# Two attention blocks in one kernel: scores of even and odd heads issued in turn into two PSUM banks, and one PSUM pool of eight banks

## The chip, the cores and the metric

The kernel runs on one core of a Trainium2 chip. Times are device microseconds of one launch; the time of a kernel is the median of its runs. The engines are TensorE (PE in the profile, with its weight loads as PEld), VectorE (DVE), ScalarE (ACT), GpSimd (POOL) and SyncE (SP), which here issues the loads. PSUM, into which PE writes its products, has eight banks of 128 x 512 float32.

## The reference

The input x has 256 tokens of width 1024. Two residual networks run one after the other, each with two layers; all of it is float32.

```python
def first_block(x, ...):
    for l in range(2):
        x = x + 0.5 * swiglu(rms_norm(x, norm_ffn1[l]), ...)
        x = x + hybrid_mixer(rms_norm(x, norm_mix[l]), ...)   # 12 dilated softmax heads, 4 stick-breaking heads
        x = x + 0.5 * swiglu(rms_norm(x, norm_ffn2[l]), ...)
    return rms_norm(x, norm_final)

def second_block(x, ...):
    for l in range(2):
        proj = rms_norm_2(x, norm_mix_pre[l]) @ w_in[l]
        # o_a: attention over compressed, selected and windowed keys (8 heads)
        # o_b: conformer, 31 taps, layer norm; o_c: pooling; o_d: sliding-window attention with sinks (8 heads)
        up = einsum("bsnc,ncd->bsnd", stack([o_a, o_b, o_c, o_d]), w_branch[l])
        mix = einsum("bsnd,bsnd->bsd", sigmoid(h @ w_gate[l]), up) @ w_o[l]
        x = x + rms_norm_2(mix, norm_mix_post[l])
        x = x + rms_norm_2(gated_conv_ffn(rms_norm_2(x, norm_ffn_pre[l])), norm_ffn_post[l])
    return x
```

A head has 64 features. Per 128 queries a softmax head needs the scores q k^T (with a mask), their maximum, the exponential, and the product with v.

## The kernel before

The tokens are two tiles of 128 (t = 0, 1). Every weight is loaded as float32 in chunks of 128 x 1024 (`chunk`), which ACT rounds to `wh` (L110) and DVE completes by `wl` (L111); a product with a weight is three matmuls into a tile called `lin`: L184 to L186 (`mm3`, 128 x 512) or L203 to L205 (`lin_T`, 128 x 256). `kouter` runs the products with the down and output weights, half of the columns after the other; behind each half stands the residual or the norm, and `head` makes `xg`, x times the gain of the next norm (L1026), which `transposed` turns by four matmuls with the identity (L155).

Everything else that PE does goes into tiles called `aux`: transposes, scores, products with v, statistics. An attention (`attend1` in the first block, `attn` in the second, where `AHEAD` lets the scores run two groups ahead of the outputs) works by heads: the mask by a bf16 matmul (L415, L458, L519 to L523), the score products (L421, L464, L527; for the compressed keys L810), DVE's maximum (L423, L530), ACT's exponential (L432, L539), transposes of `e` (L155), a copy to SBUF (L436, L547), the products with v (L449, L553). A head's 64 features of q and k lie on partitions 0 to 63 if the head is even and 64 to 127 if it is odd; a score product so uses 64 rows of PE's array (64*128 in the rows below) where all others use 128.

The program is written in one sequence, layer by layer. A scheduler of the tile framework decides the order on each engine: it starts an instruction when what it needs is there, and it gives a tile a buffer of its tag in the order in which the program asks for it. PSUM has two tags, four banks each:

```python
psum = ctx.enter_context(tc.tile_pool(name="psum", bufs=4, space=bass.MemoryType.PSUM))
psum.tile([P, 512], F32, tag="lin", name=nm("lin"))
psum.tile([P, 512], F32, tag="aux", name=nm("aux"))
```

So `lin` tiles that stand later in the program can be filled while `aux` tiles of an attention wait for DVE or ACT. The functions that the change touches, with what calls them:

Of the kernel before, what the change touches and what calls it, by code (L numbers as in the profile page):

```python
# [8 lines left out]
F32 = mybir.dt.float32  # L9
# [6 lines left out]
P = 128  # L16
# [9 lines left out]
def body(tc, ctx, I, C, out, upto=99):  # L26
# [9 lines left out]
    psum = ctx.enter_context(tc.tile_pool(name="psum", bufs=4, space=bass.MemoryType.PSUM))  # L36
# [14 lines left out]
    def lin_ps():  # L51
        return psum.tile([P, 512], F32, tag="lin", name=nm("lin"))

    def aux_ps():
        return psum.tile([P, 512], F32, tag="aux", name=nm("aux"))
# [47 lines left out]
    # ---- weights: float32 as loaded, split into two float32r parts that add up to it  # L103
# [63 lines left out]
    def split_T(tag, srcs, scale=None):  # L167
        """[128 tokens, 512] blocks -> XT of their transposes (one or two blocks)."""
# [25 lines left out]
    def lin_T(xts, ws, blks, ps=None, ks=range(8)):  # L194
        """Transposed products: [128 columns of the weights, all tokens] blocks, two to a PSUM bank."""
# [12 lines left out]
    def row_scale(xts):  # L208
        """The tokens' 1/rms along the free axis, on every partition."""
# [71 lines left out]
    class Halves:  # L281
        """XT of both token tiles, split half by half as the blocks come."""
# [9 lines left out]
    # ---- block 1  # L292
    def ffn1(xts, tail, wg, wu, wd):
        hts = [XT(), XT()]
        rb = None
        for nb in range(6):
# [9 lines left out]
            else:  # L306
                # the first half of the features first: the other half's norm may still be under way
# [71 lines left out]
    def attend1(qkn, vs):  # L379
        QT = [None, None]  # L380
        oTs = []
        for t in range(2):
# [26 lines left out]
            for j in range(4):  # L409
                groups = [[0, 1, 2]] if t == 0 else [[0, 1], [2]]  # L410
                ps_l, mx, sm = [], stat(4), stat(4)
                for gi, gs in enumerate(groups):
                    n = len(gs) * nk * P
                    ps = aux_ps()[:, :n]
                    nc.tensor.matmul(ps, identb, dilm[t][:, gs[0]:gs[-1] + 1, :].rearrange("p g k -> p (g k)"),  # L415
                                     start=True, stop=False)
                    for gg in gs:
                        h = gg * 4 + j
                        for kt in range(nk):
                            c0 = ((gg - gs[0]) * nk + kt) * P  # L420
                            nc.tensor.matmul(ps[:, c0:c0 + P], qk(h, False, t), qk(h, True, kt), start=False,  # L421
                                             stop=(gg == gs[-1] and kt == nk - 1))
                    V.tensor_reduce(mx[:, gi:gi + 1], ps, op=OP.max, axis=AX.X)  # L423
                    ps_l.append(ps)
# [26 lines left out]
            # stick-breaking heads, keys on partitions: log w = z - sum over j >= s of softplus(z_j)  # L451
# [3 lines left out]
            for par in range(2):  # L455
                o = par * 64
                z = aux_ps()[:, :n]
                nc.tensor.matmul(z[:, n - 256:], identb, sbm[:, None, :].to_broadcast([P, 2, P]), start=True, stop=False)  # L458
                for kt in range(nk):
                    for jj in range(2):  # L460
# [3 lines left out]
                        nc.tensor.matmul(z[:, c0:c0 + P], k_, q_, start=False, stop=(kt == nk - 1 and jj == 1))  # L464
                S.activation(es[par], z, AF.Abs)
                zs.append(z)
# [39 lines left out]
    def attn(t, qT, kTf, vf, window, sink=None):  # L506
        """softmax attention of 8 heads over the keys up to the query; returns the unnormalised output and the sums."""
# [4 lines left out]
        def scores(h0):  # L512
            par = h0 % 2
            hs = list(range(h0, h0 + 2 * per, 2))
            n = per * nk * P
            ps = aux_ps()[:, :n]
            pv = ps.rearrange("p (h k) -> p h k", h=per)
            if t == 0:
                nc.tensor.matmul(pv, identb, swm[:, None, P:].to_broadcast([P, per, P]), start=True, stop=False)  # L519
            elif window:  # L520
                nc.tensor.matmul(pv, identb, swm[:, None, :].to_broadcast([P, per, 2 * P]), start=True, stop=False)
            else:
                nc.tensor.matmul(pv[:, :, P:], identb, swm[:, None, P:].to_broadcast([P, per, P]), start=True, stop=False)  # L523
            for i, h in enumerate(hs):
                q_ = qT[par * 64:par * 64 + 64, (h // 2) * P:(h // 2 + 1) * P]
                for kt in range(nk):
                    nc.tensor.matmul(pv[:, i, kt * P:(kt + 1) * P], q_, kTf(kt, h), start=False,  # L527
                                     stop=(i == per - 1 and kt == nk - 1))
            sl = slice(h0, h0 + 2 * per - 1, 2)
            V.tensor_reduce(mx[:, sl], pv, op=OP.max, axis=AX.X)  # L530
            if sink is None:
                V.tensor_scalar(ng[:, sl], mx[:, sl], -0.125, None, op0=OP.mult)  # L532
            else:
                V.scalar_tensor_tensor(mx[:, sl], mx[:, sl], 0.125, sink[:, sl], op0=OP.mult, op1=OP.max)
                V.tensor_scalar(ng[:, sl], mx[:, sl], -1.0, None, op0=OP.mult)
            e = unit("e")[:, :n]
            ev = e.rearrange("p (h k) -> p h k", h=per)
            for i, h in enumerate(hs):
                S.activation(ev[:, i], pv[:, i], AF.Exp, bias=ng[:, h:h + 1], scale=0.125, accum_out=dn[:, h:h + 1])  # L539
            return h0, e  # L540
# [14 lines left out]
        # the scores run one group ahead of the outputs  # L555
        ahead = []
        po = None
        for par in range(2):
            for h0 in range(par, 8, 2 * per):
                ahead.append(scores(h0))  # L560
                if po is None:
                    po = aux_ps()
                if len(ahead) > AHEAD:
                    output(*ahead.pop(0))
# [15 lines left out]
    def mixer2(xts, tail, l):  # L580
# [8 lines left out]
        # pooling branch  # L589
# [45 lines left out]
        # token blocks for the compressed keys and values  # L635
# [22 lines left out]
        # conformer branch: gated input, transposed, 31 taps  # L658
# [15 lines left out]
        # compressed keys and values  # L674
# [35 lines left out]
        # projections of the attention branches  # L710
# [17 lines left out]
        # compressed keys (transposed) and values (block diagonal over the heads)  # L728
# [23 lines left out]
        # rotated keys, on both halves of the partitions  # L752
# [29 lines left out]
        # sliding window with sinks  # L782
# [13 lines left out]
        # native sparse attention: compressed, selected and window parts  # L796
        oA = []
        for t in range(2):
# [8 lines left out]
            for par in range(2):  # L807
                ps = aux_ps()[:, :64].rearrange("p (i n) -> p i n", i=4)
                for i in range(4):
                    nc.tensor.matmul(ps[:, i], qu[par * 64:par * 64 + 64, i * P:(i + 1) * P],  # L810
                                     kcT[par * 64:par * 64 + 64, (i // 2) * 16:(i // 2) * 16 + 16],
                                     start=i == 0, stop=i == 3)
                V.tensor_tensor(sc[:, par], ps, cmpm[t][:, None, 0:16].to_broadcast([P, 4, 16]), op=OP.add)
# [27 lines left out]
        def conformer():  # L841
            # convolution along the tokens (channels on partitions)
# [7 lines left out]
            # layer norm over the channels and silu of the conformer branch  # L850
# [27 lines left out]
        # gated sum of the branches  # L878
# [37 lines left out]
    def ffn2(xts, tail, l):  # L916
# [6 lines left out]
        for nb in range(6):  # L923
# [9 lines left out]
            for which in range(2):  # L933
# [8 lines left out]
                for t in range(0 if nb else 2):  # L942
                    # by token tiles, so that the second one's norm may still be under way
# [31 lines left out]
    # ---- the chain of sublayers: each ends, per token tile, with the norm that opens the next one  # L975
# [113 lines left out]
def layouts(inputs):  # L1089
    """Small per-channel parameters laid out with the channels on partitions."""  # L1090
# [44 lines left out]
```

## Time and profile before

| what | us |
|---|---|
| median of 3 runs (2186.62 to 2187.11) | 2186.66 |
| span of the profiled execution | 2183.6 |
| PE busy in it | 2154.8 |
| DVE busy | 1498.1 |
| ACT busy | 1111.1 |
| POOL busy | 37.2 |

The profiled execution is told by its span, from the first instruction to the end; the timed runs lie 3.1 us above it, in what stands around the span. A float32 matmul of 128 columns appears as two instructions in the trace (two passes), so counts of score products and of transposes are twice those of the code.

### The profile page before, as it was taken

The numbers are of one execution on the slowest core, as the hardware profiler recorded it, in microseconds if no ns is written. First come the engines' busy times: TensorE is split into PE (matmuls) and PEld (weight loads), VectorE is DVE, ScalarE is ACT, GpSimd is POOL, SyncE is SP. The second block draws the span as 40 slices with busy tenths as digits, with TensorE's granted clock in tenths as the row PEclk, the third lists the DMA queues.
The fourth block names the chain that finished last, engine by engine and source line by source line (L and its number), as shares of the span: only waits on it lengthen the run. The fifth ranks groups of instructions, "written<-read, shape, count | busy, mean of one in ns | idle before, by whom it ended". The sixth has DMA issues, their size and how long they took to land.

```text
span 2183.6 us, 33552 instructions
## 1 busy us (share of the span) xinstructions
PE 2154.8 (99%) x13232; PEld 1900.9 (87%) x13232; DVE 1498.1 (69%) x2219; ACT 1111.1 (51%) x1590; POOL 37.2 (2%) x55
## 2 busy tenths in 40 slices
PE   7999999999999999999999999999999999999998
PEld 7998888999899888889987888888987888888997
DVE  5665456665566555476657997668976898577983
ACT  4444545444444455544445654447655554446662
POOL 0000000000000000000000000000000000000000
PEclk9999999999999999999999999999999999999999
DMA  8656534665665654366566642456666743355653
GB/s 258 184 186 181 193 115 127 185 190 184 194 183 174 198 186 146 94 195 182 172 199 188 213 132 86 134 176 207 182 192 198 210 139 118 110 183 173 185 176 124
DMA packets 210126, 374.02 MB, mean 171 GB/s; under 512 B 15024, under 2 KB 42032, under 8 KB 209968
## 3 DMA queue, kind: packets, MB, share of 16 engines
q1 hardware_dynamic: 209392, 371.48, 55.3%
q8 instruction: 104, 1.70, 0.3%
q0 software_dynamic: 576, 0.39, 0.1%
q14 instruction: 54, 0.44, 0.1%
HBM read 371.17 MB, written 1.05 MB: 170 GB/s over the span
## 4 chain that ended last, share of the span: by engine, by line
PE 95%; DVE 3%; POOL 1%; issue 1%; ACT 1%; DMA 0%; SPq 0%; POOLq 0%; DVEq 0%
PE lin L186 17%; PE lin L184 17%; PE lin L185 17%; PE lin L203 11%; PE lin L204 11%; PE lin L205 11%; PE aux L155 4%; PE aux L527 2%; PE aux L553 1%; PE aux L421 1%; DVE wl L111 1%; PE aux L449 1%; DVE xg L1026 0%; POOL st L255 0%; DMA x<-in_x_dram 0%
## 5 line engine op out<-in xcount | busy, mean ns | idle before, releaser
L111 DVE TENSOR_TENSOR wl<-raw,wh 128x1024 fp32r<-128x1024 f32 (+1 forms) x688 | 834.9, 1217 | 467.6 <-ACT wh L110 459.0
L110 ACT ACTIVATE wh<-raw 128x1024 fp32r<-128x1024 f32 (+1 forms) x688 | 723.5, 1055 | 672.8 <-PE lin L186 325.0
L203 PE MATMUL lin<-hi,wh 128*128 128x256 f32 x1984 | 563.0, 284 | 0.0
L204 PE MATMUL lin<-lo,wh 128*128 128x256 f32 x1984 | 562.6, 284 | 0.0
L205 PE MATMUL lin<-hi,wl 128*128 128x256 f32 x1984 | 562.2, 283 | 0.0
L186 PE MATMUL lin<-wh,lo 128*128 128x512 f32 (+2 forms) x1376 | 536.1, 390 | 1.5 <-DVE rs L1037 0.9
L184 PE MATMUL lin<-wh,hi 128*128 128x512 f32 (+2 forms) x1376 | 536.7, 391 | 0.0
L185 PE MATMUL lin<-wl,hi 128*128 128x512 f32 (+2 forms) x1376 | 534.6, 389 | 1.5 <-DVE wl L111 1.5
L204 PEld LDWEIGHTS lin<-lo,wh 128*128 128x128 f32 x1984 | 381.8, 192 | 0.2
L203 PEld LDWEIGHTS lin<-hi,wh 128*128 128x128 f32 x1984 | 381.8, 192 | 0.2
L205 PEld LDWEIGHTS lin<-hi,wl 128*128 128x128 f32 x1984 | 381.6, 192 | 0.0
L186 PEld LDWEIGHTS lin<-wh,lo 128*128 128x128 f32 x1376 | 258.6, 188 | 54.1 <-DVE lo L147 2.6
L185 PEld LDWEIGHTS lin<-wl,hi 128*128 128x128 f32 x1376 | 258.7, 188 | 51.3 <-DVE wl L111 1.9
L184 PEld LDWEIGHTS lin<-wh,hi 128*128 128x128 f32 x1376 | 258.6, 188 | 50.7 <-ACT wh L110 0.4
L847 DVE SCALAR_TENSOR_TENSOR cy<-cT,pm,cy 128x251 f32<-128x251 f32 (+17 forms) x240 | 101.4, 463 | 0.2
L959 DVE SCALAR_TENSOR_TENSOR fy<-fu,fc,fy 128x255 f32<-128x255 f32 (+1 forms) x176 | 72.0, 477 | 0.2
L186 PE MATMUL lin<-wh,fl 128*128 128x512 f32 x176 | 68.6, 390 | 0.0
L184 PE MATMUL lin<-wh,fh 128*128 128x512 f32 x176 | 68.5, 389 | 0.0
L185 PE MATMUL lin<-wl,fh 128*128 128x512 f32 x176 | 68.5, 389 | 0.0
L539 ACT ACTIVATE e<-aux,st 128x128 f32<-128x128 f32 (+1 forms) x96 | 39.0, 422 | 42.3 <-DVE st L532 30.0
L255 POOL TENSOR_TENSOR st<-st,half 128x1 f32<-128x1 f32 x28 | 27.4, 979 | 1674.8 <-DVE st L254 1673.5
L957 ACT ACTIVATE fy<-fu,fc 128x256 f32<-128x256 f32 x88 | 45.7, 589 | 0.6 <-DVE fu L941 0.6
(303 smaller groups left out, 1956.9 us busy)
## 6 DMA issues: line engine op xcount, KB each, us to landing
raw<-in_ffn_w_up_dram SPq DMA_DIRECT2D x160, 512.0 KB, 4.1
raw<-in_ffn_w_down_dram SPq DMA_DIRECT2D x132, 512.0 KB, 4.3
raw<-in_w_in_dram SPq DMA_DIRECT2D x132, 512.0 KB, 4.0
raw<-in_ffn_w_gate_dram SPq DMA_DIRECT2D x80, 512.0 KB, 4.3
raw<-in_w_gate_dram SPq DMA_DIRECT2D x64, 512.0 KB, 3.9
raw<-in_w_branch_dram SPq DMA_DIRECT2D x32, 512.0 KB, 4.6
raw<-in_ffn_w_up_dram SPq DMA_DIRECT2D x32, 256.0 KB, 3.3
raw<-in_w_out_dram SPq DMA_DIRECT2D x16, 512.0 KB, 4.2
```

The source lines that it names most:

```text
L110: S.activation(wh, raw, AF.Copy)
L111: V.tensor_sub(wl, raw, wh.bitcast(F32))
L155: nc.tensor.transpose(p[:, i * P:(i + 1) * P], s, ident)
L184: nc.tensor.matmul(ps, xt.h[k], w[0], start=start, stop=False)
L185: nc.tensor.matmul(ps, xt.h[k], w[1], start=False, stop=False)
L186: nc.tensor.matmul(ps, xt.l[k], w[0], start=False, stop=stop)
L203: nc.tensor.matmul(o, wh, xh, start=k == 0 and i % 2 == 0, stop=False)
L204: nc.tensor.matmul(o, wh, xl, start=False, stop=False)
L205: nc.tensor.matmul(o, wl, xh, start=False, stop=k == 7 and i % 2 == 1)
L847: V.scalar_tensor_tensor(y4[:, c, sh:], c4[:, c, :T - sh], cw[:, j * 4 + c:j * 4 + c + 1], y4[:, c, sh:], op0=OP.mult, op1=OP.add)
L957: S.activation(y4[:, c], u4[:, c], AF.Identity, scale=fc[:, f0 + 2:f0 + 3], bias=fc[:, f0 + 3:f0 + 4])
L959: V.scalar_tensor_tensor(y4[:, c, sh:], u4[:, c, :T - sh], fc[:, f0 + 2 - sh:f0 + 3 - sh], y4[:, c, sh:], op0=OP.mult, op1=OP.add)
```

## The change

The two tags become one with eight buffers. In all attentions the score products of two groups of heads, an even and an odd one, are issued in turn, each group into a bank of its own; before, a group was finished before the next was begun. In the first block a pair of heads (j = 0, 1 and j = 2, 3) has both its scores made first, and then goes through exponential, transposes, copy and output one after the other. The number of products is the same.

```diff
-    psum = ctx.enter_context(tc.tile_pool(name="psum", bufs=4, space=bass.MemoryType.PSUM))
+    psum = ctx.enter_context(tc.tile_pool(name="psum", bufs=8, space=bass.MemoryType.PSUM))
     def lin_ps():
-        return psum.tile([P, 512], F32, tag="lin", name=nm("lin"))
+        return psum.tile([P, 512], F32, tag="ps", name=nm("lin"))
     def aux_ps():
-        return psum.tile([P, 512], F32, tag="aux", name=nm("aux"))
+        return psum.tile([P, 512], F32, tag="ps", name=nm("aux"))
...
+            def scores(js):
+                r = [([], stat(4), stat(4)) for _ in js]
                 for gi, gs in enumerate(groups):
                     n = len(gs) * nk * P
-                    ps = aux_ps()[:, :n]
-                    nc.tensor.matmul(ps, identb, dilm[t][:, gs[0]:gs[-1] + 1, :].rearrange("p g k -> p (g k)"),
-                                     start=True, stop=False)
+                    pss = [aux_ps()[:, :n] for _ in js]
+                    for ps in pss:
+                        nc.tensor.matmul(ps, identb, dilm[t][:, gs[0]:gs[-1] + 1, :].rearrange("p g k -> p (g k)"),
+                                         start=True, stop=False)
                     for gg in gs:
                         for kt in range(nk):
                             c0 = ((gg - gs[0]) * nk + kt) * P
+                            for ps, j in zip(pss, js):
+                                h = gg * 4 + j
+                                nc.tensor.matmul(ps[:, c0:c0 + P], qk(h, False, t), qk(h, True, kt), start=False,
+                                                 stop=(gg == gs[-1] and kt == nk - 1))
...
+            for js in ((0, 1), (2, 3)):
+                for j, r in zip(js, scores(js)):
+                    output(j, *r)
...
-            for i, h in enumerate(hs):
-                q_ = qT[par * 64:par * 64 + 64, (h // 2) * P:(h // 2 + 1) * P]
+            for i in range(per):
                 for kt in range(nk):
+                    for par, pv in enumerate(pvs):
+                        h = h0 + 2 * i + par
+                        q_ = qT[par * 64:par * 64 + 64, (h // 2) * P:(h // 2 + 1) * P]
+                        nc.tensor.matmul(pv[:, i, kt * P:(kt + 1) * P], q_, kTf(kt, h), start=False,
+                                         stop=(i == per - 1 and kt == nk - 1))
```

The stick-breaking heads and the compressed keys (L810 before) are changed in the same way. The order on PE, at the first head of the first layer's attention (query tile 0; lin_3029 is a tile of the gates' product, which stands behind the attention in the program). Before:

```order
L421 MATMUL aux_2624<-qt_2595 128x128 [waits Activation_49]
L421 MATMUL aux_2624<-qt_2596,qt_2595 128x128 [waits DVE_49]
L421 MATMUL aux_2624<-qt_2596,qt_2595 128x128
L186 MATMUL lin_3029<-wh_3007,lo_1845 128x512
L184 MATMUL lin_3029<-wh_3007,hi_1844 128x512
L185 MATMUL lin_3029<-wl_3008,hi_1844 128x512
L186 MATMUL lin_3029<-wh_3007,lo_1845 128x512
L184 MATMUL lin_3029<-wh_3013,hi_1844 128x512
L185 MATMUL lin_3029<-wl_3014,hi_1844 128x512
L186 MATMUL lin_3029<-wh_3013,lo_1845 128x512
L184 MATMUL lin_3029<-wh_3013,hi_1844 128x512
L155 MATMUL aux_2633<-ident,e_2631 128x128 [waits Activation_49]
```

The same place after the change (aux_2626 is head 0's bank, aux_2627 head 1's):

```order
L425 MATMUL aux_2626<-qt_2595 128x128 [waits DVE_49,Activation_49]
L425 MATMUL aux_2627<-qt_2595 128x128
L425 MATMUL aux_2626<-qt_2596,qt_2595 128x128 [waits DVE_49]
L425 MATMUL aux_2627<-qt_2596,qt_2595 128x128
L425 MATMUL aux_2626<-qt_2596,qt_2595 128x128
L425 MATMUL aux_2627<-qt_2596,qt_2595 128x128
L155 MATMUL aux_2641<-ident,e_2639 128x128 [waits Activation_49]
L155 MATMUL aux_2641<-ident,e_2639 128x128 x2
L457 MATMUL aux_2648<-v_2117,pt_2645 128x64 [waits DVE_49]
L457 MATMUL aux_2648<-v_2117,pt_2645 128x64 x2
L155 MATMUL aux_2656<-ident,e_2654 128x128 [waits Activation_49]
L155 MATMUL aux_2656<-ident,e_2654 128x128 x2
```

Between the scores and the transposes of `e` that need their exponential stood eight `lin` matmuls; now none stands there, nor between the transposes and the products with v. It is so in all four attentions: from the first transposes of q and k to the last of the output PE's order holds no `lin` matmul (186 matmuls of the code in a row in each layer of the first block, 294 in each of the second).

The order on PE behind the first half of the first sublayer's down product (the transposes of xg for the next sublayer; lin_1871 and lin_1872 are the second half of the columns). Before:

```order
L184 MATMUL lin_1872<-wh_1875,hi_438 128x512 [waits PE_49]
L185 MATMUL lin_1872<-wl_1876,hi_438 128x512
L155 MATMUL aux_1848<-ident,xg_1846 128x128 [waits DVE_49]
L155 MATMUL aux_1848<-ident,xg_1846 128x128 x3
L186 MATMUL lin_1872<-wh_1875,lo_439 128x512
L155 MATMUL aux_1861<-ident,xg_1859 128x128 [waits DVE_49]
```

After:

```order
L185 MATMUL lin_1641<-wl_1705,hi_1630 128x512
L186 MATMUL lin_1641<-wh_1704,lo_1631 128x512
L155 MATMUL aux_1848<-ident,xg_1846 128x128 [waits DVE_49,PE_49]
L155 MATMUL aux_1848<-ident,xg_1846 128x128 x3
L155 MATMUL aux_1861<-ident,xg_1859 128x128 [waits DVE_49,PE_49]
L155 MATMUL aux_1861<-ident,xg_1859 128x128 x3
L184 MATMUL lin_1871<-wh_1875,hi_438 128x512 [waits Activation_49]
```

The eight matmuls of the second half that stood ahead of the transposes now stand behind them, and the transposes follow the last matmul on whose product xg depends (lin_1641).

The order on PE at the layer norm of the conformer, second block, first layer (L860 and L867 before are L881 and L888 after). Before:

```order
L184 MATMUL lin_13305<-wh_13315,hl_12039 128x512
L860 MATMUL aux_13278<-avg,sq_13276 128x1 [waits PE_49,Activation_49]
L860 MATMUL aux_13278<-avg,sq_13276 128x1 x7
L185 MATMUL lin_13305<-wl_13316,hl_12039 128x512
L186 MATMUL lin_13305<-wh_13315,hl_12039 128x512
L867 MATMUL aux_13291<-ident,st_13289 128x128 [waits PE_49,Pool_49]
```

After:

```order
L186 MATMUL lin_13120<-wh_13090,lo_10950 128x512
L874 MATMUL aux_13270<-cy_11353,avg 128x256 x4
L881 MATMUL aux_13278<-avg,sq_13276 128x1 [waits Activation_49]
L881 MATMUL aux_13278<-avg,sq_13276 128x1 x7
L888 MATMUL aux_13291<-ident,st_13289 128x128 [waits Pool_49]
L888 MATMUL aux_13291<-ident,st_13289 128x128
L184 MATMUL lin_13305<-wh_13309,hl_12039 128x512
```

The three steps of the statistics follow each other directly; 16 `lin` matmuls stood between the first and the second, two between the second and the third.

## Rows read from the trace of the kernel before

**Rows 1.** The page: span, busy times, and TensorE's granted clock in 40 slices.

```profile
span 2183.6 us, 33552 instructions
...
PE 2154.8 (99%) x13232; PEld 1900.9 (87%) x13232; DVE 1498.1 (69%) x2219; ACT 1111.1 (51%) x1590; POOL 37.2 (2%) x55
...
PEclk9999999999999999999999999999999999999999
...
L255 POOL TENSOR_TENSOR st<-st,half 128x1 f32<-128x1 f32 x28 | 27.4, 979 | 1674.8 <-DVE st L254 1673.5
```

**Rows 2.** The waits of PE over the span: total us, times, longest us.

```profile
PE aux L155 <- DVE xg L1026: 15.0, 9, 7.6
PE aux L749 <- POOL hv L745: 2.3, 2, 1.4
```

**Rows 3.** Windows over one attention stretch of each block: busy us of every engine.

```profile
272.00:353.00 81.00, 81.00 (x467) 65.19 (x466) 41.51 (x86) 42.15 (x71) 0.00 (x0) 1.00 0.34 104
...
1257.00:1378.00 121.00, 120.91 (x729) 99.78 (x728) 99.02 (x218) 62.26 (x153) 0.00 (x0) 1.00 0.33 105
```

**Rows 4.** The same two windows, instructions on aux tiles alone: PE, PEld, DVE, ACT.

```profile
272.00:353.00 81.00, 43.09 (x295) 34.60 (x280) 19.81 (x39) 16.04 (x41) 1.00 0.34 104
...
1257.00:1378.00 121.00, 62.07 (x452) 50.48 (x434) 27.26 (x44) 30.81 (x114) 1.00 0.33 105
```

**Rows 5.** Timeline of one head of query tile 0: start, us, engine, line.

```profile
280.34 0.48 PE L421 MATMUL aux<-qt 64*128 64x128 f32 x2
280.66 0.61 PE L421 MATMUL aux<-qt,qt 64*128 64x128 f32 x4
...
281.31 0.56 DVE L423 TENSOR_REDUCE st<-aux 128x1 f32<-128x384 f32 x1 [0.74 <-PE aux L421]
...
282.15 0.58 ACT L432 ACTIVATE e<-aux,st 128x384 f32<-128x384 f32 x1 [4.28 <-DVE st L427]
...
282.94 0.49 PE L155 MATMUL aux<-ident,e 128*128 128x128 f32 x3
...
283.47 0.56 DVE L436 COPY pt<-aux 128x384 f32<-128x384 f32 x1 [0.45 <-PE aux L155]
...
284.20 0.78 PE L449 MATMUL aux<-v,pt 128*128 128x64 f32 x6
```

**Rows 6.** Groups by line and form, window 272 to 353 (first block's attention).

```profile
L436 DVE COPY pt<-aux 128x512 f32<-128x512 f32 x4 | 2.8, 692 | 4.4 <-PE aux L155 4.4
L423 DVE TENSOR_REDUCE st<-aux 128x1 f32<-128x512 f32 x4 | 2.7, 687 | 1.8 <-PE aux L421 1.8
...
L468 ACT ACT_TABLE_LOAD x2 | 2.6, 1283 | 0.0
L475 ACT ACT_TABLE_LOAD x2 | 2.6, 1283 | 0.0
...
L467 ACT ACTIVATE se<-se 128x1024 f32<-128x1024 f32 x1 | 1.1, 1059 | 0.0
```

**Rows 7.** Groups by line and form, window 1257 to 1378 (second block's attentions).

```profile
L527 PE MATMUL aux<-kT,qT 64*128 64x128 f32 x96 | 14.4, 287 | 0.0
...
L539 ACT ACTIVATE e<-aux,st 128x256 f32<-128x256 f32 x24 | 11.1, 470 | 15.3 <-DVE st L532 9.2 <-PE aux L155 3.5 <-DVE st L534 2.6
L539 ACT ACTIVATION_READ_ACCUMULATOR e<-aux,st 128x1 f32 x48 | 9.9, 206 | 0.0
...
L530 DVE TENSOR_REDUCE st<-aux 128x2 f32<-128x512 f32 x12 | 8.3, 689 | 4.4 <-PE aux L527 4.4
```

**Rows 8.** The chain that ended last, two of its pieces: start, us, what.

```profile
307.73 1.08 PE aux L421 x8
...
322.43 1.42 PE aux L449 x12
```

**Rows 9.** Windows around the conformer's statistics: busy us of PE, PEld, DVE, ACT, POOL, then the granted clock.

```profile
1393.00:1397.00 4.00, 3.54 (x26) 2.83 (x25) 0.85 (x2) 1.36 (x2) 0.70 (x1) 1.00 0.39 140
1397.00:1401.00 4.00, 4.00 (x13) 3.14 (x12) 3.74 (x8) 1.21 (x2) 0.00 (x0) 0.57 0.00 0
1401.00:1405.00 4.00, 4.00 (x20) 3.29 (x19) 3.59 (x5) 2.81 (x3) 0.00 (x0) 1.00 0.48 139
```

**Rows 10.** Groups by line and form, window 1378 to 1485 (steps behind the second block's attentions).

```profile
L255 POOL TENSOR_TENSOR st<-st,half 128x1 f32<-128x1 f32 x4 | 4.0, 1004 | 82.6 <-DVE st L254 82.6
L277 DVE SCALAR_TENSOR_TENSOR x<-po,st,x 128x512 f32<-128x512 f32 x4 | 2.8, 748 | 1.2 <-POOL st L255 1.2
...
L1026 DVE TENSOR_TENSOR xg<-x,gn 128x512 f32<-128x512 f32 x4 | 2.6, 682 | 0.0
...
L856 ACT ACTIVATE sq<-cy 128x1024 f32<-128x1024 f32 x1 | 1.1, 1060 | 2.4 <-DVE cy L854 2.4
```

More of the change, by code (lines that the diff above doesn't have):

```diff
@@ L408, in attend1, with output @@
             oc = unit("oc")
-            for j in range(4):
-                groups = [[0, 1, 2]] if t == 0 else [[0, 1], [2]]
-                ps_l, mx, sm = [], stat(4), stat(4)
+            groups = [[0, 1, 2]] if t == 0 else [[0, 1], [2]]
+            def scores(js):
+                r = [([], stat(4), stat(4)) for _ in js]
                 for gi, gs in enumerate(groups):
                     n = len(gs) * nk * P
-                    ps = aux_ps()[:, :n]
-                    nc.tensor.matmul(ps, identb, dilm[t][:, gs[0]:gs[-1] + 1, :].rearrange("p g k -> p (g k)"),
-                                     start=True, stop=False)
+                    pss = [aux_ps()[:, :n] for _ in js]
+                    for ps in pss:
+                        nc.tensor.matmul(ps, identb, dilm[t][:, gs[0]:gs[-1] + 1, :].rearrange("p g k -> p (g k)"),
+                                         start=True, stop=False)
                     for gg in gs:
-                        h = gg * 4 + j
                         for kt in range(nk):
                             c0 = ((gg - gs[0]) * nk + kt) * P
[L421 to L424, printed above, removed]
+                            for ps, j in zip(pss, js):
+                                h = gg * 4 + j
+                                nc.tensor.matmul(ps[:, c0:c0 + P], qk(h, False, t), qk(h, True, kt), start=False,
+                                                 stop=(gg == gs[-1] and kt == nk - 1))
+                    for ps, (ps_l, mx, sm) in zip(pss, r):
+                        V.tensor_reduce(mx[:, gi:gi + 1], ps, op=OP.max, axis=AX.X)
+                        ps_l.append(ps)
+                return r
+            def output(j, ps_l, mx, sm):
                 if len(groups) == 2:
@@ L455, in attend1 @@
             for par in range(2):
-                o = par * 64
                 z = aux_ps()[:, :n]
                 nc.tensor.matmul(z[:, n - 256:], identb, sbm[:, None, :].to_broadcast([P, 2, P]), start=True, stop=False)
-                for kt in range(nk):
-                    for jj in range(2):
+                zs.append(z)
+            for kt in range(nk):
+                for jj in range(2):
+                    for par in range(2):
+                        o = par * 64
                         k_ = QT[kt][1][o:o + 64, (6 + jj) * P:(7 + jj) * P]
@@ L463, in attend1 @@
                         c0 = kt * 256 + jj * P
-                        nc.tensor.matmul(z[:, c0:c0 + P], k_, q_, start=False, stop=(kt == nk - 1 and jj == 1))
-                S.activation(es[par], z, AF.Abs)
-                zs.append(z)
+                        nc.tensor.matmul(zs[par][:, c0:c0 + P], k_, q_, start=False, stop=(kt == nk - 1 and jj == 1))
+            for par in range(2):
+                S.activation(es[par], zs[par], AF.Abs)
             S.activation(e2[:, :2 * n], e2[:, :2 * n], AF.Exp, scale=-1.0)
@@ L512, in scores @@
         def scores(h0):
-            par = h0 % 2
-            hs = list(range(h0, h0 + 2 * per, 2))
             n = per * nk * P
[L516 to L523, printed above, removed]
@@ L524, in scores @@
-            for i, h in enumerate(hs):
-                q_ = qT[par * 64:par * 64 + 64, (h // 2) * P:(h // 2 + 1) * P]
-                for kt in range(nk):
[L527 to L540, printed above, removed]
+            pvs = []
+            for _ in range(2):
+                pv = aux_ps()[:, :n].rearrange("p (h k) -> p h k", h=per)
+                if t == 0:
+                    nc.tensor.matmul(pv, identb, swm[:, None, P:].to_broadcast([P, per, P]), start=True, stop=False)
+                elif window:
+                    nc.tensor.matmul(pv, identb, swm[:, None, :].to_broadcast([P, per, 2 * P]), start=True, stop=False)
+                else:
+                    nc.tensor.matmul(pv[:, :, P:], identb, swm[:, None, P:].to_broadcast([P, per, P]), start=True, stop=False)
+                pvs.append(pv)
@@ new lines, in scores @@
+            for i in range(per):
+                for kt in range(nk):
+                    for par, pv in enumerate(pvs):
[3 more added lines that the diff above has]
+                                         stop=(i == per - 1 and kt == nk - 1))
+            r = []
+            for par, pv in enumerate(pvs):
+                hs = list(range(h0 + par, h0 + 2 * per, 2))
+                sl = slice(h0 + par, h0 + par + 2 * per - 1, 2)
+                V.tensor_reduce(mx[:, sl], pv, op=OP.max, axis=AX.X)
+                if sink is None:
+                    V.tensor_scalar(ng[:, sl], mx[:, sl], -0.125, None, op0=OP.mult)
+                else:
+                    V.scalar_tensor_tensor(mx[:, sl], mx[:, sl], 0.125, sink[:, sl], op0=OP.mult, op1=OP.max)
+                    V.tensor_scalar(ng[:, sl], mx[:, sl], -1.0, None, op0=OP.mult)
+                e = unit("e")[:, :n]
+                ev = e.rearrange("p (h k) -> p h k", h=per)
+                for i, h in enumerate(hs):
+                    S.activation(ev[:, i], pv[:, i], AF.Exp, bias=ng[:, h:h + 1], scale=0.125, accum_out=dn[:, h:h + 1])
+                r.append((h0 + par, e))
@@ L542, in output @@
+            return r
         def output(h0, e):
@@ L557, in attn @@
         po = None
[L558 to L564, printed above, removed]
+        for h0 in range(0, 8, 2 * per):
+            ahead += scores(h0)
+            if po is None:
+                po = aux_ps()
+            while len(ahead) > AHEAD:
+                output(*ahead.pop(0))
         for g in ahead:
@@ L806, in mixer2 @@
             s8 = sc.rearrange("p a i n -> p (a i) n")
-            for par in range(2):
-                ps = aux_ps()[:, :64].rearrange("p (i n) -> p i n", i=4)
-                for i in range(4):
+            pss = [aux_ps()[:, :64].rearrange("p (i n) -> p i n", i=4) for _ in range(2)]
+            for i in range(4):
+                for par, ps in enumerate(pss):
                     nc.tensor.matmul(ps[:, i], qu[par * 64:par * 64 + 64, i * P:(i + 1) * P],
@@ L812, in mixer2 @@
                                      start=i == 0, stop=i == 3)
+            for par, ps in enumerate(pss):
                 V.tensor_tensor(sc[:, par], ps, cmpm[t][:, None, 0:16].to_broadcast([P, 4, 16]), op=OP.add)
```

## The prediction

> **What bounds the kernel now.** I read the page first, then PE's waits, then windows, timeline and chain. PE is busy for 2154.8 of 2183.6 us, at the full granted clock in every slice [rows 1]; its largest wait, for xg, is 15.0 us in nine times, 7.6 of them at the start [rows 2]. The time is PE's work, and a change counts by what it does to that work or to its cover. The cover shows in the attentions: the window 272 to 353 has PE busy throughout [rows 3], yet the attention's own tiles account for 43.1 us of its 81 [rows 4]; the other 37.9 are `lin` matmuls laid into the waits. In the second block's window it is 62.1 of 121, so 58.9 are fill. One head shows why they fit: first score at 280.34, maximum 281.31, exponential 282.15, transposes 282.94, copy 283.47, products with v 284.20 to 284.98 [rows 5]: 4.6 us, of which the head's own matmuls take about two.
>
> **What the change moves.** Nothing is removed: the products are the same. What changes is the order. With one tag for all PSUM tiles a `lin` tile that stands later in the program gets its bank only after the `aux` tiles ahead of it have got theirs, and those wait for their heads. So each attention is now an unbroken run of dependent steps, and so is every transpose, statistic or pooling step elsewhere whose input comes from DVE, ACT or POOL. The `lin` work that filled these waits is done afterwards, in full. Each stretch costs its chain's length less its own PE work. VectorE and ScalarE still split weights ahead, but only until their six buffers are full, so no work replaces the cover.
>
> **First block's attentions (two).** The times of the steps are those of rows 5 and 6, with some 0.1 us at each handover as between the rows of 5. *A pair of heads, tile 0:* two masks and 12 score passes 1.9; two maxima 2 x 0.56, scaling, the first exponential 0.58 and handovers 2.2; then, for each head in turn, transposes to products with v 283 to 285 in rows 5, that is 1.9 to 2.0. Sum 8.0, two pairs 16.0. *Stick-breaking, tile 0:* scores, two absolute values, exponential, table load 1.28, logarithm, sum, product with ntri, exponential, output: 8.6. *A pair, tile 1:* the scores of 24 passes in two steps 3.7 (eight passes take 1.08, [rows 8]), maxima and first exponential 2.6 (0.69 for 512 columns, [rows 6]), and 3.05 for each head's transposes, two copies and 12 products (1.42, [rows 8]): 12.4, two pairs 24.8. *Stick-breaking, tile 1:* the same steps at 1.06 for 1024 columns: 11.5. With 2.8 and 3.0 for the transposes and copies of q and k ahead, 66.7 us, less 43.1: **23.6 each, 47 in both layers**.
>
> **Second block's attentions (two).** The same steps with eight heads: a maximum 0.69, and an exponential 0.47 with 0.21 for its sum, 48 of them in the window [rows 7], so that ACT's row of exponentials is the longest piece of each chain. By the same adding up the two sliding-window tiles take 12.4 and 14.6, the sparse attention's tiles, each with the compressed softmax (some ten steps of 0.2 to 0.6) and two attentions, 29 and 32: 88, less 62.1: 26. VectorE's queue holds convolution steps of the conformer between these (up to 12 in a row ahead of the first maximum), for which I add 6. **32 each, 64**.
>
> **The other steps.** *xg:* behind each half of a sublayer's last product PE now waits for the residual and xg, 0.7 and 0.68 each [rows 10], for two tiles: 2.0 us. Twelve such halves in the first block make 24, less 5 that stand in before's waits already [rows 2]: 19. *The gated sum of the first block's mixer:* two halves with two steps of 0.6 to 0.7 ahead of the transposes, 5.5 a layer: 11. *The second block's mixer outside attention:* channel input 2, pooling 8 (adds and multiplications on four groups one after the other), duplicated keys 3.2, gated conformer input 4.4, compression 8.5 (POOL's copies, ropes and two rounds of transposes), layer norm 4.5 (ACT 1.06 for the squares, POOL's power 0.98, [rows 1, 10]), gated sum 5: 35.6 a layer, 71. *Between mixer and feed-forward:* POOL's power 1.00, x 0.75, xg 0.68 and the next transposes [rows 10], for four halves and their following `fn` steps: 12 a layer, 24, and 8 where the next mixer begins. **133** together. These I hold for the least certain, since they were hidden in before and so have no wait to be read from.
>
> **The clock.** Where PE's work thinned out in before, the granted clock fell: from 1393 to 1397 PE issued 16 one-column matmuls and waited 0.46, and the next four microseconds ran at 0.57 [rows 9], part of them at 1.2 GHz instead of 2.4; four microseconds of dense `lin` were back at full clock. The stick-breaking step holds 4 to 6 us in which PE does nothing at all, and so does the compressed softmax. I take the clock as halved from there to the end of the attention: matmuls of some 22 us in each of the first block's and 38 in each of the second's take that much again, **120** in all. The bounds are nothing, if the clock stays up or returns between heads, and 210, the double of all attention work [rows 4] in four stretches. The Trainium skill, "TensorE: Matmul & The Clock Gate", HAM oscillation, says that waits between bursts of matmuls bring the half clock back each time; rows 9 agree for one place.
>
> **What alternating gives.** Before, a group of eight score passes takes 1.08 [rows 8], 135 ns a pass, where passes on all 128 rows take 118 (1.42 for 12, the same rows): entering and leaving the group costs about 0.1 to 0.2. Fewer groups are already in the chains. Whether two halves of the array work at once no row of before shows, since neighbours always use the same half. The lower bound is nothing; the upper one is half of the 480 score passes (in each layer 72 of dilated and 24 of stick-breaking heads, 96 of the sparse [rows 7] and 48 of the sliding-window attention) at some 0.11 us, 27 us. No row is nearer to either, and I take **13** off. The Trainium skill, "TensorE: Matmul & The Clock Gate", Part 3 (The mechanism), states that weight loads run beside a matmul only where their row groups differ, as they now do; by that the sum would have 27 in place of 13. It states nothing against the waits, which are ten times as large.
>
> **The sum.** 2186.7 + 47 + 64 + 133 + 120 - 13 = 2537.7, told as **2540** us. The profiled span would be 3 less.
>
> **The rivals.** *The clock stays up.* PE has work in more than half of each attention (43 of 67, 62 of 88), and the full clock held in all slices before. Then the 120 falls away: about 2420. For it speaks that rows 9 show one short fall only; against it the empty stretches. *The waits are smaller than summed.* Steps may overlap where I laid them end to end, the next pair's scores or the second tile's copies slipping into the first's waits, and half of the small steps may meet no wait. Half of 244, and half the clock's price: 2187 + 122 + 60 - 13, about 2355. *The change doesn't do what it says,* the two halves still going one after the other: 13 more, 2553, inside the main case. *Faster.* If the order costs nothing, because the scores were the only work that could not be filled, alternating gives up to 27 and the saved group switches 7: 2153. It decides only if the chains' waits are below 34 us in all; against it stand 37.9 and 58.9 us of fill in rows 3 and 4, four times over, which must now stand elsewhere. *No change* would need these to cancel.
>
> **How the numbers follow.** The main case has 0.55, with 2470 to 2640 for itself; the full clock 0.18; smaller waits 0.22; faster 0.03, and within 0.2% (about what a measurement of this kernel can tell from no change) 0.02. The range of eight in ten reaches from the smaller waits to the main case's upper end: 2340 to 2640. Slower by over 0.2% is 0.95.
>
> **What would show it.** PE's busy share of the attention windows falls to some 60%, with waits for `e` (DVE, ACT) between scores, transposes and products with v, and no `lin` row between the first and the last of them; PE's waits for xg rise to some 35 us; the granted clock shows slices of 5 to 8 tenths at the four attentions and 9 elsewhere; score passes of a pair stand under 110 ns apart if both halves work. Wrong would be: `lin` matmuls inside the attentions on the chip, waits under 150 us in all, or a clock that falls between the attentions too, in which case even 2640 is too low.

## The result, and the profile after

The changed kernel takes **2550.49 us** (2550.06 to 2550.86, 4 runs) where the kernel before takes 2186.89 beside it: a ratio of 1.1662, 95% interval 1.1648 to 1.1676. It is 364 us slower; 2540 was forecast, in a range of 2340 to 2640. The page of its profiled execution, against [rows 1]:

```profile
span 2548.3 us, 33507 instructions
...
PE 2258.7 (89%) x13232; PEld 1972.1 (77%) x13232; DVE 1511.3 (59%) x2219; ACT 1123.4 (44%) x1590; POOL 33.9 (1%) x55
...
PEclk9999779999999969999888679999998867999999
```

PE was idle for 28.8 us of its span before (2183.6 less 2154.8) and is for 289.6 now: 261 us more. It is also busy for 103.9 us longer with the same 13232 matmuls. Both together are the 364.7 us by which the span grew. The clock row, all nines before, has dips to 6, 7 and 8 tenths in twelve slices. PE's waits, against [rows 2] (us in total, times, longest us):

```profile
PE aux L155 <- DVE xg L1047: 59.4, 21, 7.8
PE aux L155 <- ACT e L559: 22.9, 12, 4.2
PE aux L155 <- DVE qr L518: 21.4, 8, 4.4
PE aux L640 <- DVE sA L631: 20.6, 2, 10.5
PE aux L485 <- DVE se L484: 18.3, 4, 5.3
PE aux L155 <- ACT e L440: 16.6, 8, 2.2
PE aux L574 <- DVE pt L568: 12.6, 12, 2.3
PE aux L155 <- DVE kd L518: 12.5, 4, 3.6
```

None of these but xg stood in the list of before. Five of them are steps of an attention (e twice, qr, se, pt), three are not (xg, the pooling's sA, the keys kd). The four attentions as windows, from the first transposes to the last, all engines (PE, PEld, DVE, ACT, POOL busy, then the granted clock); they answer to [rows 3, 4]:

```profile
276.90:350.70 73.80, 51.94 (x284) 41.12 (x282) 25.51 (x72) 25.27 (x52) 0.00 (x0) 0.63 0.09 28
894.00:968.40 74.40, 52.45 (x284) 41.56 (x282) 25.49 (x72) 25.47 (x52) 0.00 (x0) 0.63 0.09 28
1408.30:1521.60 113.30, 77.48 (x457) 59.88 (x458) 60.35 (x159) 32.87 (x119) 0.00 (x0) 0.66 0.02 7
2050.30:2163.20 112.90, 77.69 (x457) 60.10 (x458) 60.44 (x159) 32.76 (x119) 0.00 (x0) 0.66 0.02 8
```

The same windows counted on aux tiles alone give PE 51.90 in the first: no `lin` work is left inside. PE is busy for 69% of these 374.4 us, and its granted clock of 0.63 to 0.66 means that it ran at 1.2 GHz for some seven tenths of them. Weights are hardly split there any more: DVE's step for them (L111) has 2.4 us in each of the first two windows and nothing in the other two, where it had 17.7 and 27.9 us in the windows of [rows 3].

One pair of heads (timeline: start, us, line), against [rows 5]. A score product and a product with v are two instructions each in the trace, a transpose is one (x3 for the three blocks of `e`), so that counts of transposes are those of the code and not twice them:

```profile
279.80 0.61 PE L425 MATMUL aux<-qt,qt 64*128 64x128 f32 x8
280.44 1.02 DVE L428 TENSOR_REDUCE st<-aux 128x1 f32<-128x384 f32 x2
...
281.62 0.58 ACT L440 ACTIVATE e<-aux,st 128x384 f32<-128x384 f32 x1 [1.71 <-DVE st L435]
...
282.34 0.55 PE L155 MATMUL aux<-ident,e 128*128 128x128 f32 x3 [1.93 <-ACT e L440]
...
282.93 0.56 DVE L444 COPY pt<-aux 128x384 f32<-128x384 f32 x1 [0.44 <-PE aux L155]
283.54 0.97 PE L457 MATMUL aux<-v,pt 128*128 128x64 f32 x6 [0.65 <-DVE pt L444]
```

The brackets are the cover that is gone: PE waits 1.93 for the exponential and 0.65 for the copy, where `lin` matmuls stood. The first row shows the other half of the change: eight passes take 0.61, as four did before.

### The profile page after: what moved, and what is told of

It is laid out like the page before. It is cut to its first block, busy times and chain, and to the rows that moved or that the text cites. A ratio compares the mean times of both kernels' runs of the same rounds, so it can differ in the third digit from the quotient of the medians.

```text
span 2548.3 us, 33507 instructions
## 1 busy us (share of the span) xinstructions
PE 2258.7 (89%) x13232; PEld 1972.1 (77%) x13232; DVE 1511.3 (59%) x2219; ACT 1123.4 (44%) x1590; POOL 33.9 (1%) x55
## 5 line engine op out<-in xcount | busy, mean ns | idle before, releaser
L111 DVE TENSOR_TENSOR wl<-raw,wh 128x1024 fp32r<-128x1024 f32 (+1 forms) x688 | 837.1, 1218 | 633.5 <-ACT wh L110 617.9
L184 PE MATMUL lin<-wh,hi 128*128 128x512 f32 (+2 forms) x1376 | 541.2, 393 | 0.0
L184 PEld LDWEIGHTS lin<-wh,hi 128*128 128x128 f32 x1376 | 264.1, 192 | 51.7
L868 DVE SCALAR_TENSOR_TENSOR cy<-cT,pm,cy 128x233 f32<-128x233 f32 (+19 forms) x240 | 98.5, 462 | 0.3
L155 PE MATMUL aux<-ident,xg 128*128 128x128 f32 x160 | 31.5, 342 | 67.3 <-DVE xg L1047 59.4
L155 PE MATMUL aux<-ident,e 128*128 128x128 f32 x216 | 49.6, 363 | 39.6 <-ACT e L559 22.9
L155 PEld LDWEIGHTS aux<-ident,xg 128*128 128x128 f32 x160 | 22.6, 174 | 77.9 <-issue 65.6
L155 PEld LDWEIGHTS aux<-ident,e 128*128 128x128 f32 x216 | 35.0, 193 | 48.7 <-ACT e L559 30.3
```

The lines of the kernel that those rows point to most:

```text
L111: V.tensor_sub(wl, raw, wh.bitcast(F32))
L155: nc.tensor.transpose(p[:, i * P:(i + 1) * P], s, ident)
L184: nc.tensor.matmul(ps, xt.h[k], w[0], start=start, stop=False)
L868: V.scalar_tensor_tensor(y4[:, c, sh:], c4[:, c, :T - sh], cw[:, j * 4 + c:j * 4 + c + 1], y4[:, c, sh:], op0=OP.mult, op1=OP.add)
```

## The experiments

**The two parts, each alone.** alt_two_tags keeps the alternating scores and gives back the two tags:

```diff
-        return psum.tile([P, 512], F32, tag="ps", name=nm("lin"))
+        return psum.tile([P, 512], F32, tag="lin", name=nm("lin"), bufs=4)
-        return psum.tile([P, 512], F32, tag="ps", name=nm("aux"))
+        return psum.tile([P, 512], F32, tag="aux", name=nm("aux"), bufs=4)
```

> The changed kernel with its alternating scores, but with the two tags of before, four banks each. Theory (one tag for all PSUM tiles takes the cover away, alternating itself saves): the waits go, about 2187 less 27 (480 score passes at half their pitch) and some 5 for group switches, 2150 to 2165 us, PE busy 99%. Rival (the scores made by pairs leave nothing between them, whatever the banks): most of the 364 us stay, above 2300 us.

Measured: 2159.97 us, ratio to before 0.9873 (0.9858 to 0.9888). The rival falls: without the common tag the same order of scores is **27 us faster** than before. Page and waits:

```profile
span 2157.2 us, 33561 instructions
...
PE 2124.9 (99%) x13232; PEld 1869.9 (87%) x13232; DVE 1493.9 (69%) x2219; ACT 1109.1 (51%) x1590; POOL 36.4 (2%) x55
```

```profile
PE aux L155 <- DVE xg L1047: 14.2, 9, 8.6
PE aux L155 <- ACT e L559: 4.1, 6, 0.8
```

All waits of the changed kernel but 4.1 us for e and those of before are gone, and PE's busy time is 29.9 below that of before.

old_scores_one_tag is the kernel before with one tag of eight banks:

```diff
-    psum = ctx.enter_context(tc.tile_pool(name="psum", bufs=4, space=bass.MemoryType.PSUM))
+    psum = ctx.enter_context(tc.tile_pool(name="psum", bufs=8, space=bass.MemoryType.PSUM))
-        return psum.tile([P, 512], F32, tag="lin", name=nm("lin"))
+        return psum.tile([P, 512], F32, tag="ps", name=nm("lin"))
-        return psum.tile([P, 512], F32, tag="aux", name=nm("aux"))
+        return psum.tile([P, 512], F32, tag="ps", name=nm("aux"))
```

> The kernel before with its old order of scores, all PSUM tiles on one tag of eight banks. Theory (the tag alone): as slow as the changed kernel or slower by what alternating saves, 2560 to 2610 us. Rival (alternating is what costs): 2187 to 2200 us.

Measured: 2630.42 us, ratio 1.2025 (1.1997 to 1.2053). The tag alone makes the kernel 443 us slower, more than the 2560 to 2610 us expected: the new order of scores gives back 80 us of it, three times what it gives with two tags. The first attention of old_scores_one_tag, as a window (columns as above):

```profile
277.80:371.80 94.00, 67.43 (x285) 52.51 (x284) 27.02 (x72) 26.02 (x52) 0.00 (x0) 0.58 0.07 22
```

It lasts 94.0 us against 73.8, PE is busy for 67.4 against 51.9, at a clock of 0.58 against 0.63. The four attentions together last 456.0 us against 374.4, so the 80 us lie in them.

**Where the cover is lost.** others_own_banks lets only the attentions share banks with `lin` (aux tiles outside them have a tag of three banks, attentions and lin five); attention_own_banks is its counterpart (attentions and the row scale four of their own, all other aux tiles share four with lin):

```diff
+    where = ["own"]
-        return psum.tile([P, 512], F32, tag="ps", name=nm("lin"))
+        return psum.tile([P, 512], F32, tag="ps", name=nm("lin"), bufs=5)
-        return psum.tile([P, 512], F32, tag="ps", name=nm("aux"))
+        return psum.tile([P, 512], F32, tag=where[0], name=nm("aux"), bufs=5 if where[0] == "ps" else 3)
...
+        where[0] = "ps"
         oTs = attend1(qk, vs)
+        where[0] = "own"
```

(The same two switches stand around the attentions of the second block; in attention_own_banks the two tags are the other way round.)

> The changed kernel, but the aux tiles outside the attentions have three banks of their own; attentions share five with lin. So only the attentions lose their cover. By the terms of the prediction 2187 + 47 + 64 + 120 - 13, about 2405 us; by the four stretches in the trace of the changed kernel (375 us where their tiles took 210 before) 2187 + 165, about 2352 us.

> The counterpart of others_own_banks: the attentions (and the row scale) have four banks of their own, all other aux tiles share four with lin. So the attentions keep their cover, with alternating scores, and only the other dependent steps lose it. By the terms of the prediction 2187 + 133 - 27, about 2293 us; by the difference of the runs so far (2550 less 2374, plus 2160) about 2336 us.

Measured: 2374.52 us (ratio 1.0854, 1.0832 to 1.0876) and 2338.85 us (1.0696, 1.0674 to 1.0717). Over alt_two_tags that is 215 us for the attentions' cover and 179 for that of the other steps; together 393, where the changed kernel lies 391 above. The parts add up. The first lies between the two figures expected for it (2405 and 2352 us); the second meets the one from the runs (2336) and is 46 us above the one from the terms of the prediction (2293), which held no price of the clock for these steps. PE over the whole of the two (window: PE busy first, clock behind POOL):

```profile
0.00:2374.00 2374.00, 2227.95 (x13232) 1953.31 (x13232) 1503.19 (x2219) 1117.78 (x1590) 37.72 (x55) 0.94 0.51 158
```

```profile
0.00:2336.00 2336.00, 2169.11 (x13229) 1901.05 (x13232) 1502.96 (x2219) 1116.28 (x1590) 32.70 (x55) 0.97 0.53 160
```

PE idles for 146.4 us in the first (span 2374.3) and 166.7 in the second (2335.8), against 32.3 in alt_two_tags: 114 us of waits for the attentions, 134 for the rest. What else was lost, 103 and 44 us, is longer busy time of PE. The waits of attention_own_banks:

```profile
PE aux L157 <- DVE xg L1056: 58.7, 21, 8.8
PE aux L646 <- DVE sA L637: 20.4, 2, 10.3
PE aux L157 <- DVE kd L524: 12.6, 4, 3.6
PE aux L157 <- DVE gd L377: 9.1, 6, 2.8
PE aux L157 <- ACT fn L975: 8.8, 8, 2.3
PE aux L157 <- DVE bin L696: 8.6, 4, 2.2
PE aux L157 <- DVE st L258: 7.8, 2, 4.0
PE aux L890 <- ACT sq L886: 7.0, 2, 3.5
PE aux L157 <- DVE gt L929: 6.1, 4, 1.6
...
PE aux L897 <- POOL st L894: 2.1, 2, 1.0
```

**Alternating, or pairing?** The change does two things to the scores: it makes them by pairs of groups, and it alternates inside a pair. two_tags_not_alternated and one_tag_not_alternated keep the pairs and undo the alternation, on two tags and on one:

```diff
-            for i in range(per):
-                for kt in range(nk):
-                    for par, pv in enumerate(pvs):
+            for par, pv in enumerate(pvs):
+                for i in range(per):
+                    for kt in range(nk):
```

(the same in the other attentions).

> As alt_two_tags, masks and scores by pairs into two banks, but the products of the even group all ahead of those of the odd one. Theory (two halves of the array at once): the 27 us come back, 2180 to 2187 us. Rival (pairs of masks and fewer switches between 64 and 128 rows are the gain): stays at 2160 to 2165 us.

> The changed kernel, one tag of eight banks, with the products of the even group ahead of those of the odd one. If the halves of the array working at once are what the changed kernel has over old_scores_one_tag (2630 us; aux tiles busy 467 us against 379): most of the 80 us come back, 2600 to 2630 us. If it is the chain by pairs of heads: 2550 to 2575 us.

Measured: 2171.59 us (0.9929, 0.9912 to 0.9945) and 2556.07 us (1.1689, 1.1666 to 1.1713). With two tags neither theory holds alone: pairing gives 15 us (2186.6 to 2171.6) and alternating 11.6 more. With one tag the second one does: pairing gives 74 (2630.4 to 2556.1) and alternating 6. Sixteen score passes of the sliding-window attention's first tile as the timelines show them, in two_tags_not_alternated and in alt_two_tags:

```profile
1270.33 1.71 PE L544 MATMUL aux<-dkT,qT 64*128 64x128 f32 x16
```

```profile
1261.02 1.16 PE L544 MATMUL aux<-dkT,qT 64*128 64x128 f32 x16
```

In this tile the kernel before had its even and its odd group next to each other already, and took the same 1.71 for them:

```profile
1258.70 1.71 PE L527 MATMUL aux<-dkT,qT 64*128 64x128 f32 x16
```

So here all of the gain comes from alternating. Where a mask or `lin` matmuls stood between the groups, eight passes of one took 1.16 before (last section), two such groups 2.32, and pairing alone can bring the two closer.

With one tag alternating shortens PE's busy time by 22 us (2281.0 in one_tag_not_alternated, 2258.7 in the changed kernel) but lengthens its waits by 15 (274.4 to 289.6). The waits for `e` do it, 23.7 us there and 39.5 in the changed kernel (16.6 and 22.9 above):

```profile
PE aux L155 <- ACT e L440: 13.1, 8, 2.0
...
PE aux L155 <- ACT e L559: 10.6, 8, 2.7
```

Alternating finishes both groups at the end of the pair, so that the first maximum can't start while the second group's products run; that this is why the waits grow was not tested by itself.

**More banks for aux.** alt_3_and_5 is alt_two_tags with bufs=3 for lin and 5 for aux.

> alt_two_tags with three banks for lin and five for aux. The waits for e and pt there are 4.5 us in all, so more aux banks can give 5 at most: 2155 to 2160 us. If the feed-forward's four lin tiles need their four banks: 2165 to 2190 us, with waits at L203.

Measured: 2163.39 us (0.9898, 0.9883 to 0.9912), 3.4 above alt_two_tags, at the edge of what these runs can tell. It lies between the two ranges expected. The fifth bank brings nothing: the waits for e are 5.5 us in place of 4.1, and 2.7 us of waits at L184 for the evacuation of a `lin` bank (L688) are new. The feed-forward's products did not show up as a wait.

**The clock.** fill_waits lays products that nobody reads into the waits of the attentions, and fill_lean the same in smaller pieces (256 columns, other counts):

```diff
+    def fill(n, src):
+        for _ in range(n):
+            nc.tensor.matmul(dps, ident, src[:, :512], start=True, stop=True)
...
+                fill(3 if t == 0 else 4, QT[t][0])
...
+            fill(8 if t == 0 else 12, QT[t][0])
...
+                fill(3, qT)
...
+            fill(4, qu)
```

(Behind a pair's scores, the stick-breaking scores, the first scores of `attn` and the compressed scores.)

> The changed kernel with float32 products of 512 columns, read by nobody, laid into the waits of its four attentions (one of the eight banks is given to them); adds work, leaves none out. If the half clock in the attentions costs what the PE rows say (aux tiles busy 379 us where they took 307): the clock stays up there and the time falls by 50 to 90, to 2460 to 2500 us. If the slower passes lie in waits that would be there anyway: within 20 of 2550 us, or above by what the added products cost.

> As fill_waits, with products of 256 columns and about half of the added work, so that less of it outlasts the waits. If the half clock costs PE some 100 us in the attentions (others_own_banks: busy 2228 against 2125 in alt_two_tags) and the added work stood in the way in fill_waits: 2490 to 2520 us. If passes at half clock are hidden in waits: 2530 to 2550 us, as fill_waits or above.

Measured: 2530.75 us (1.1568, 1.1545 to 1.1591) and 2536.25 us (1.1593, 1.1560 to 1.1627). Adding work made the kernel 20 and 14 us faster. Both times lie in the range of the second expectation, that the slower passes are hidden in waits (for fill_waits at its very edge), and miss that of the first by 31 and 16 us. The windows show more than the totals. The first attention of fill_waits, all engines, then aux and fill tiles alone (PE, PEld and so on; clock third from the end):

```profile
277.70:344.80 67.10, 64.58 (x352) 41.56 (x350) 25.54 (x72) 25.45 (x52) 0.00 (x0) 0.95 0.09 31
...
277.70:344.80 67.10, 36.67 (x282) 29.38 (x265) 18.95 (x38) 15.28 (x41) 0.95 0.09 31
...
277.70:344.80 67.10, 32.93 (x68) 11.54 (x68) 0.95 0.09 31
```

The clock stayed up (0.95 for 0.63), and the attention's own passes fell from 51.9 to 36.7 us, by 15. The stretch shortened by 6.7 only, and PE is now busy for 64.6 of 67.1: the added products outlast the waits. In the second layer's attention the clock stayed full, its own passes took 33.8 us, and the stretch 64.2 where it took 74.4:

```profile
887.70:951.90 64.20, 61.68 (x352) 38.75 (x350) 25.47 (x72) 25.39 (x52) 0.00 (x0) 1.00 0.10 33
```

In the second block the clock came back to 0.84 and 0.78 alone; the one stretch is 4.0 us shorter, the other 3.3 longer. The four together are 17.6 us shorter, nearly all of the 19.0 by which the span fell. So part of the slower passes lies on the path; how much time a full clock without added work would give back stays open.

## Why the prediction was right

**The cover.** The step on which everything rests, that a common tag puts `lin` behind the attentions' tiles and that each dependent step is then paid for, is shown by the two runs with one part each: 2160 us with the new scores alone, 2630 with the tag alone. The rival that the change would be faster was right about the sign of the scores (34 us told with the saved group switches, 27 measured with the tags kept) and failed at the point that it named: the waits are not below 34 us.

**The waits in the attentions** were put at 47 + 64, 111 us; others_own_banks has 114. In the profile after PE is idle for 44 us in the first block's two windows, where 47 was told, and for 71 in the second block's, where 64 was. The pair of tile 0, summed to 8.0, takes 8.45 from its masks to those of the next pair (278.69 to 287.14); between its last score pass and its transposes stand 1.93, where the steps had 2.2:

```profile
278.69 0.49 PE L418 MATMUL aux<-dilm,identb 128*128 128x384 bf16 x2
...
284.30 0.85 PE L155 MATMUL aux<-ident,e 128*128 128x128 f32 x3
285.80 1.54 PE L457 MATMUL aux<-v,pt 128*128 128x64 f32 x6 [0.65 <-DVE pt L444]
287.14 0.85 PE L418 MATMUL aux<-dilm,identb 128*128 128x384 bf16 x2
...
288.50 1.06 PE L425 MATMUL aux<-qt,qt 64*128 64x128 f32 x8
```

The first head's steps, 282.34 to 284.30, are the 1.9 to 2.0 of the sum; the second's, at a lower clock, take 2.8.

**The other waits**, which I held for the least certain, were put at 133; attention_own_banks has 134. Inside, the pooling has 20.4 (16 forecast), the gated input 8.6 (8.8), the layer norm's squares with POOL's power 9.1 (7.0 and 2.1; 9 forecast), the gates of the first block 9.1 (11). The nearness of the total owes something to chance: xg stands at 59.4 us in the profile after where the text named 35, while the gated sum of the second block has 6.1 where 10 was put.

**The clock** term is where the sum was mis-sized, in its place rather than its total. It gave 120 us to the attentions and nothing to the rest. Busy time grew by 103 us in the attentions and by 44 outside them. The window 1366 to 1381 of the profile after, the compression and its keys, shows the second part:

```profile
1366.20:1381.00 14.80, 5.27 (x27) 4.40 (x26) 12.94 (x26) 3.90 (x9) 2.39 (x4) 0.62 0.54 174
```

PE is busy for 5.3 of 14.8 us there at a clock of 0.62. Not all of the longer busy time is the clock: a matmul with no neighbour shows its whole length as busy. The pair above tells the two apart in one place. With `lin` around them a head's transposes took 0.49 and its products with v 0.78 [rows 5]; alone, at full clock, the first head's take 0.55 and 0.97; alone, at half clock, the second's take 0.85 and 1.54. Of the 1.12 us by which these two steps grew, 0.87 are the clock, which falls about where the first head ends:

```profile
278.00:284.00 6.00, 3.13 (x29) 2.30 (x28) 4.36 (x10) 3.14 (x7) 0.00 (x0) 1.00 0.87 290
284.00:290.00 6.00, 4.92 (x27) 3.60 (x26) 1.60 (x5) 0.00 (x0) 0.00 (x0) 0.52 0.00 1
```

For the whole of the 103 and 44 us this was not separated. What the text named as a way to be wrong, a clock that falls between the attentions too, did happen, but not with the consequence that it told (over 2640 us): the longer busy time outside them is 44 us in all. The rival of a clock that stays up (2420 us) is out, with 0.63 to 0.66 in all four; so is that of smaller waits, which wanted half of 244 where 248 were measured.

**Alternating** was given 13 us of a possible 27. With two tags the new scores are worth 27, but by two causes, 15 for pairs and 11.6 for alternating; with one tag pairs are worth 74. The prediction had the pairs in its chains and gave no figure for the tag with the old order, which is worse still. In the changed kernel itself alternating is worth 6, not 13. The text also says that no row of before shows whether two halves work at once, since neighbours always use the same half. That is wrong: in the first tile of the sliding-window attention the two halves are neighbours, and sixteen passes took 1.71 us (1258.70, above), 107 ns each, where a group alone took the 135 ns of the text. So the lower bound of nothing, and the rival of two halves going one after the other, had a row of before against them.

With the measured terms the sum is 2187 + 114 + 134 + 103 + 44 - 27 = 2555, against 2550. Of the forecast's 120 - 13, the first was 27 too small and the second 14: the two errors cancel by half.

**What was wrong** in the list of signs: PE's busy share in the attentions is 69%, not 60; its waits for xg are 59.4 us, not 35; and the clock row has five slices of 8 tenths outside the attentions, where all were to be at 9. The waits for `e` inside the attentions, the missing `lin` rows and the distance of the score passes (eight in 0.61 us) were as told.

## What to carry to other kernels

Where a scheduler hands out buffers of one tag in program order, a tag is also a statement about what may overtake what: work that is to fill another's waits needs buffers of its own. Read from the windows what fills a stretch before touching it (81 us here, of which the attention's tiles took 43), and price its loss as the chain's length less its own work, and the slower clock of an engine with holes on top. The two parts of this change pull opposite ways; the better kernel takes the scores and leaves the tags (alt_two_tags, 2160 us, 1.3% below before and 15% below the change).

## What the runs showed of the hardware that was not expected

Score products on the two halves of the array's rows do run side by side. In the kernel before, its timeline has eight passes of one group in the time in which alt_two_tags has sixteen of a pair (1261.02, above):

```profile
1346.90 1.16 PE L527 MATMUL aux<-kT,qT 64*128 64x128 f32 x8
```

Even without alternation two adjacent groups of opposite halves take 1.71 in place of two times 1.16, in the kernel before (1258.70) as in two_tags_not_alternated.

In the profile after the granted clock fell in all four attentions, and in short stretches outside them (0.62 from 1366 to 1381, with PE busy for 5.3 of 14.8 us). It did not fall in every stretch with waits. The end of the third attention, where PE is busy for 16.6 of 21.6 us, ran at full clock:

```profile
1500.00:1521.60 21.60, 16.63 (x153) 14.26 (x154) 11.60 (x28) 9.91 (x36) 0.00 (x0) 1.00 0.00 0
```

Work that nobody reads was enough to hold the clock up (0.95 for 0.63 in the first attention of fill_waits, 1.00 for 0.63 in the second).
